# Three of a unit's seven weight blocks: low part by a negated copy and an accumulating DMA; group 3's row sum one step later

## The chip, the core and the metric

The kernel runs on one core of one Trainium2 chip. A core has a matrix engine (TensorE, PE in the profile), three engines for elementwise work (VectorE or DVE, ScalarE or ACT, GpSimd or POOL), an engine that only issues transfers (SyncE or SP), and 16 DMA engines. Each of these works through its own queue in program order and waits on semaphores for the others; the kernel's author places every instruction by hand. A transfer is issued from SP's queue or from POOL's.

The metric is the device time of one execution in microseconds (us). The kernel before takes 1879.46 us (median of 3 runs, 1878.98 to 1880.03).

## The reference

One layer of a backbone on 2048 tokens of 1024 channels, in float32: a gated short convolution, then a mixture of 16 experts with expert-choice routing.

```python
m_l = (silu_c @ ada_w[i] + ada_b[i])[:, None, :]
sh1, sc1, g1, sh2, sc2, g2 = jnp.split(m_l, 6, axis=-1)
hl = modulate(rms_norm(lat, norm_g[i, 0]), sh1, sc1)
gate_b, gate_c, v = jnp.split(hl @ w_in, 3, axis=-1)
yl = (gate_b * dwconv_centred(gate_c * v, conv_w)) @ w_out
lat = lat + g1 * yl
hl2 = modulate(rms_norm(lat, norm_g[i, 1]), sh2, sc2)
lat = lat + g2 * expert_choice_ffn(hl2, moe_router[i], moe_w_gate[i], moe_w_up[i], moe_w_down[i])
```

The change lies in the first half: in the product `hl @ w_in`, and in the six vectors `sh1` to `g2` (the modulation), each the product of one vector with a 1024x1024 matrix, called groups 0 to 5 in the kernel.

## The kernel before

**Split operands.** A float32 factor is held as two tiles, a high part (the rounded value, written as float32r) and a low part (the value minus its high part). A product is three matmuls: high x high, low x high, high x low. Every weight tile therefore has a high part, made by ACT as a copy (L225, L784), and a low part, made by DVE as a subtraction (L235, L785).

**Channel loop, the first half of the tokens.** The loop at L860 runs 14 steps, i = 0 to 13; a step is one group of 128 channels for one quarter (512 tokens) of the first half, with 8 values of k and 9 matmuls each, into three PSUM banks (`in_mm`). Six banks are shared, so a step's banks are needed again two steps later, after `in_out` has emptied them. Between the values of k other work is placed by hand:

- `in_out` (L493) empties the previous step's banks: ACT copies (`cs`), DVE multiplies, POOL copies two columns of the carry, ACT and DVE do the convolution, POOL stores to DRAM.
- `split_to` makes the high and low parts of the next weight pieces (L225, L235), and each low part frees a raw buffer, for which SP then issues the next load (L200). There are three raw buffers.
- `ada_step(g, t)` (L671) does one step of the modulation of group g: at t = 0 to 7 it loads slices of the matrix (`ada_load`, tile `aw`, L528), at t = 1 to 8 DVE adds a slice times a scalar to `acc` (L540; the first by L538), and at t = 9 `ada_end` (L544) sums `acc` over the partitions by four matmul instructions with a matrix of ones (L547). In steps 0 to 4, after every odd k, comes first group 5, t = 0 to 9, then group 3, t = 0 to 9. All these loads are issued from POOL's queue. Group 3's row sum is the last one, at i = 4, k = 7.
- After step 3 `constants` makes the constants of the later routing: some 60 small operations on POOL.
- `x_step` is 5: in steps 5 and 8 the third and fourth quarter of x are loaded into the four large buffers (`b4`) that the modulation also uses, and normalised; in step 6 (`save_full`), 9 and 10 (`save_sums`) they are turned, and sums and differences of quarters are stored to DRAM (`fscr`). At the end of step 11 `load_full` begins to load these back (`fu`), through the same four buffers, in the order of `halves`; `refill` splits them into high and low parts in steps 12 and 13 and in the first four unit steps, and loads the next.

**Unit stage, the second half of the tokens.** The products for the second half are done by a scheme of seven products in place of eight (as in Strassen's): a unit takes two pieces of weights, a and b, each with two halves, and seven half-size products of blocks with the stored sums. There are 12 units, 84 unit steps. A block (`make_block`, L770) is made four unit steps before it is used (`AHEAD`). Blocks 0, 1, 4 and 6 are the halves b1, a0, a1 and b0 as they stand; blocks 2, 3 and 5 are sums, which DVE first writes over a half in place: block 2 over b1 (L778), block 3 over b1 again (L780), block 5 over a0 (L782), and with it b0 is replaced too (L783). After block 5 piece a's buffer is free, and after block 6 that of b (`piece_done`, L762), and SP issues the load of the third piece from there (L200): the buffer that a leaves takes the next unit's b. `unit_step` (L826) does the 12 matmuls of a block (L794 to L796) and empties the banks; a later block of the same unit is added into a bank after ACT has copied it out (L841).

In this stage groups 2 and 4 of the modulation run, one `ada_step` every fourth unit step, with their loads on POOL's queue, as are the convolution's stores.

Of the kernel before, what the change touches and what calls it, by code (L numbers as in the profile page):

```python
# [7 lines left out]
F32 = mybir.dt.float32  # L8
# [4 lines left out]
AF = mybir.ActivationFunctionType  # L13
ALU = mybir.AluOpType
# [8 lines left out]
KD = D // P  # L23
# [17 lines left out]
def dram(src, offset, ap):  # L41
    return bass.AP(tensor=src.tensor, offset=src.offset + offset, ap=ap)
# [3 lines left out]
def block_kernel(ctx: ExitStack, tc, x, c, ada_w, ada_b, norm_g, w_in, conv, w_out, router, wg, wu, wd, out):  # L46
    nc = tc.nc
# [195 lines left out]
    def split_to(i, eng=None):  # L243
        while n_done <= min(i, len(pieces) - 1):
            split_low(n_done, eng)
# [112 lines left out]
    with tc.tile_pool(name="mix", bufs=1) as mix, ExitStack() as ctx_mixd:  # L358

        def b4(name, shape=[P, D]):  # L360
            return mix.tile(shape, F32, name=name, tag="b4", bufs=4)

        def hl_tile(shape, dt=F32R, name="hl"):
            return mix.tile(shape, dt, name=name, tag="hl", bufs=18)
# [22 lines left out]
        def load_x(q, b0=0, b1=4):  # L387
            xq.setdefault(q, [])
            pair_ = None
            for b in range(b0, b1):  # L390
                if q == 1:
                    pair_ = big_tile([P, 2, D], F32, "xt") if b % 2 == 0 else pair_
                    t = pair_[:, b % 2]
                else:
                    t = b4("xt")
                nc.sync.dma_start(t, x[0, q * QT + b * P:q * QT + (b + 1) * P, :])
                xq[q].append(t)
# [16 lines left out]
        def scale_x(q, k):  # L414
            pt, full = pt_hl.pop((q, k)), m2("full")
            t = hl[q, k] = hl_tile([P, 2, QT])
            nc.scalar.activation(t[:, 0], pt, AF.Identity, scale=A1[:, k:k + 1], bias=sh1[:, k:k + 1])  # L417
            nc.scalar.activation(full, pt, AF.Identity, scale=A1[:, k:k + 1], bias=sh1[:, k:k + 1])
            return full
# [4 lines left out]
        def to_hl(q, k):  # L424
            turn_x(q, k)
            low_x(q, k, scale_x(q, k))
# [94 lines left out]
        def bcast_load(dst, src, off, eng=nc.sync):  # L521
            eng.dma_start(dst, dram(src, off, [[0, P], [1, D]]))
# [3 lines left out]
        def ada_load(g, k, eng=nc.sync):  # L526
            ada_in[g, k] = b4("aw")
            eng.dma_start(ada_in[g, k], ada_w[0, k * P:(k + 1) * P, g * D:(g + 1) * D])  # L528

        def ada_add(g, k, dst=None):  # L530
            t = ada_in.pop((g, k))
            if dst is None:
                if k == 0:
                    ada_dst[g] = g2b if g == 5 else b4("dst")
                dst = ada_dst[g]
            if k == 0:
                ada_acc[g] = b4("acc")
                nc.vector.tensor_scalar(ada_acc[g], t, s_col[:, 0:1], None, op0=ALU.mult)  # L538
            else:
                nc.vector.scalar_tensor_tensor(ada_acc[g], t, s_col[:, k:k + 1], ada_acc[g], op0=ALU.mult, op1=ALU.add)  # L540
            if k == 0:
                bcast_load(dst, ada_b, g * D)

        def ada_end(g, dst):  # L544
            for h in range(2):
                pt = tp.tile([P, QT], F32, name="pt", tag="tp")
                nc.tensor.matmul(pt, ones_f, ada_acc[g][:, h * QT:(h + 1) * QT], start=True, stop=True)  # L547
                nc.vector.tensor_add(dst[:, h * QT:(h + 1) * QT], pt, dst[:, h * QT:(h + 1) * QT])
            if g == 4:
                nc.vector.scalar_tensor_tensor(dst, dst, 1.0, ada_g.pop(), op0=ALU.add, op1=ALU.mult)  # L550
            if g < 5:
                nc.gpsimd.dma_start(rows[g - 2:g - 1], dst[0:1])

        def new_banks():
            return [mm.tile([P, QT], F32, name="pm", tag="mm") for _ in range(3)]
# [69 lines left out]
        for g in range(4):  # L625
            k = 2 * g
            more_g = g < 3
            ada_fix(g, 0)
            full = scale_x(0, k)
# [9 lines left out]
            full = scale_x(0, k + 1)  # L639
# [31 lines left out]
        def ada_step(g, t):  # L671

            if t == KD + 1:
                ada_end(g, ada_dst[g])
            if 0 < t <= KD:
                ada_add(g, t - 1)
            if (g, t) == (4, KD):
                ada_g.append(b4("gt"))
                bcast_load(ada_g[0], norm_g, D, nc.gpsimd)
            if t == 0:  # L680
                ada_load(g, 0, nc.gpsimd)
            if t + 1 < KD:
                ada_load(g, t + 1, nc.gpsimd)

        T4, B11, T1, T2, B21, T3, B22 = range(N_GROUP)
        group_of_k = {(2, 0): B11, (2, 1): B21, (3, 1): B22}
# [72 lines left out]
        def raw_half(i, h):  # L759
            return raws[i][:, 4 * h:4 * h + 4]  # L760

        def piece_done(i):  # L762
            nonlocal n_high, n_done
            raws.pop(i)
            n_high = n_done = i + 1
            load_to(i + depth())
# [3 lines left out]
        def make_block(n):  # L770

            u, i = divmod(n, N_GROUP)
            a, b = first_s + 2 * u, first_s + 2 * u + 1
            t = blk[n] = hl_tile([P, 2, KD // 2, P], name="sb")
            p, h = ((b, 1), (a, 0), (b, 1), (b, 1), (a, 1), (a, 0), (b, 0))[i]
            full = raw_half(p, h)
            if i == 2:
                nc.vector.tensor_add(full, raw_half(b, 0), full)  # L778
            elif i == 3:
                nc.vector.tensor_sub(full, full, raw_half(a, 0))  # L780
            elif i == 5:
                nc.vector.tensor_sub(full, full, raw_half(b, 0))  # L782
                nc.vector.tensor_sub(raw_half(b, 0), raw_half(a, 1), raw_half(b, 1))  # L783
            nc.scalar.activation(t[:, 0], full, AF.Copy)  # L784
            nc.vector.tensor_sub(t[:, 1], full, t[:, 0].bitcast(F32))  # L785
            if i > 4:
                piece_done(p)

# [67 lines left out]

        end_plain = w_chan[0, KD - 1, 2]
        steps = [(ct, q) for ct in range(KD) for q in range(2) if q or ct > 1]
        x_step = 5
        for i, (ct, q) in enumerate(steps):  # L860
            in_out(*pend)
            if i == 5:
                for t in cnts:
                    nc.vector.tensor_copy(t, zero1.to_broadcast([P, 4]))
            nxt = w_chan[0, ct, 2]
            split_to(min(end_plain, nxt + (1 if q % 2 == 0 else 3)))
            if i in (x_step, x_step + 3):
                load_x(2 if i == x_step else 3)
            last_i = len(steps) - 1
            ps = new_banks()  # L870
            for k in range(KD):
                in_mm(ps, q, W_chan(0, ct), k)
                if (ct, q) == (0, 1) and k + 3 < KD:
                    to_hl(1, k + 3)
                if i in (x_step, x_step + 3) and k in (2, 3, 4, 5):
                    norm_x(2 if i == x_step else 3, k - 2)
                if i == x_step + 1 and k % 2 == 1:
                    save_full(2, k // 2)
                if i == x_step + 3 and k == 7:
                    load_other(0)  # L880
                if i in (x_step + 4, x_step + 5) and k in (1, 5):
                    j = 2 * (i - x_step - 4) + k // 4
                    save_sums(j)
                    if j < 3:
                        load_other(j + 1)
                if i < x_step and k % 2 == 1:
                    t = 4 * i + k // 2
                    ada_step(*((5, t) if t < KD + 2 else (3, t - KD - 2)))
                if i == last_i - 2 and k == 7:
                    for s in range(4):  # L890
                        load_full(s)
                if i == last_i - 1:
                    if k in (1, 2, 4, 5, 7):
                        refill((1, 2, 4, 5, 7).index(k))
                    if k in (3, 6):
                        make_block((3, 6).index(k))
                if i == last_i:
                    if k in (1, 2, 3, 6, 7):
                        refill(5 + (1, 2, 3, 6, 7).index(k))
                    if k in (4, 5):  # L900
                        make_block(k - 2)
            pend = (ps, q, ct)
            if i == 3:
                before, ones_b, tri, slot_r, step, bias, need, zero1, cnts, aux, same, quick = constants(m2)
                nc.sync.dma_start(rt, dram(router, 0, [[E, P], [E * P, KD], [1, E]]))
                nc.scalar.activation(rts[:, :, 0], rt, AF.Copy)
                nc.vector.tensor_sub(rts[:, :, 1], rt, rts[:, :, 0].bitcast(F32))
# [22 lines left out]
        for n in range(n_steps):  # L930
            u, i = divmod(n, N_GROUP)
# [6 lines left out]
            if n >= 6 and n % 4 == 2:  # L938
                t = n // 4 - 1
# [701 lines left out]
```

## Time and profile before

| | |
|---|---|
| median of 3 runs | 1879.46 us |
| the profiled execution | 1880.41 us |
| its span in the profile | 1878.2 us |
| mean granted clock of TensorE in it | 0.986 |
| channel loop with its first part | up to about 324 us |
| unit stage | 324 to 557 us |

The span is the time from the first to the last instruction in the trace; the execution's own time lies 2.2 us above it. Two stretches of 40 us, one from the channel loop and one from the unit stage, show how the engines stand there: the length, then for PE, weight loads, DVE, ACT and POOL the busy us and the number of instructions, then the granted clock, the share of the DMA engines and GB/s.

```profile
160.00:200.00 40.00, 34.62 (x146) 27.14 (x147) 14.93 (x22) 12.16 (x18) 9.15 (x20) 0.88 0.40 129
...
400.00:440.00 40.00, 40.00 (x177) 32.94 (x177) 32.30 (x43) 15.75 (x26) 2.82 (x9) 1.00 0.35 106
```

In the first PE is idle for 5.4 us and the clock is below full; in the second PE is never idle, DVE is busy for 32 of 40 us, ACT for 16 and POOL for 3. How to read the other views: a row of the timeline has the start, the duration, the engine, the line, the operation, the tile written and the tiles read, and in brackets the idle time of the engine before it and what ended that; a row of the waits has the total, the number and the longest.

### The profile page before, as it was taken

What the parts mean: (1) busy time and instruction counts of PE and PEld (TensorE: products, weight loads), DVE (VectorE), ACT (ScalarE), POOL (GpSimd) and SP (SyncE); (2) the same over time, 40 slices, a digit from 0 to 9 for tenths busy, and PEclk for the clock granted to TensorE, in tenths of its full rate; (3) what the DMA queues carried; (4) which work ended last, traced back from release to release, by engine and by line L of the source; (5) the groups of instructions that cost most, each with busy time, mean ns of one, the idle gap of its engine ahead of it and who ended that gap; (6) DMA issues with size and microseconds to landing.
All of it is one profiled execution on the core that took longest, in us unless ns stands there. A gap on an engine that the chain in (4) does not pass through costs nothing.

```text
span 1878.2 us, 29302 instructions
## 1 busy us (share of the span) xinstructions
PE 1813.7 (97%) x11511; PEld 1609.9 (86%) x11511; DVE 1218.5 (65%) x1722; ACT 872.2 (46%) x1154; POOL 320.4 (17%) x494
## 2 busy tenths in 40 slices
PE   7998999999999999499999999999999999999998
PEld 6786888888878887398999999999999999999997
DVE  6554346777776677788666665765666576566653
ACT  5511234433344556466454554555455455444542
POOL 1223231010002222300202111210210121021002
PEclk9998999999999999799999999999999999999999
DMA  9353466434448888385778778787877978888774
GB/s 335 114 187 123 133 216 201 125 116 135 135 153 250 241 264 252 112 258 186 228 242 258 226 236 258 223 238 234 258 234 225 261 221 242 241 251 231 223 230 87
DMA packets 304634, 393.67 MB, mean 210 GB/s; under 512 B 102724, under 2 KB 173680, under 8 KB 304496
## 3 DMA queue, kind: packets, MB, share of 16 engines
q1 hardware_dynamic: 280032, 305.77, 53.3%
q0 software_dynamic: 24464, 86.03, 15.5%
q8 instruction: 90, 1.47, 0.3%
q14 instruction: 48, 0.39, 0.1%
HBM read 311.52 MB, written 57.68 MB: 197 GB/s over the span
## 4 chain that ended last, share of the span: by engine, by line
PE 87%; DVE 5%; DMA 3%; ACT 2%; issue 2%; POOL 1%; SPq 0%; POOLq 0%; DVEq 0%; ACTq 0%
PE pm L1464 12%; PE pm L1466 12%; PE pm L1468 12%; PE pm L1533 6%; PE pm L1531 6%; PE pm L1532 6%; PE pm L794 4%; PE pm L796 4%; PE pm L795 4%; PE pm L488 4%; PE pm L489 4%; PE pm L491 3%; PE pm L993 3%; PE pm L996 3%; PE pm L994 3%
## 5 line engine op out<-in xcount | busy, mean ns | idle before, releaser
L235 DVE TENSOR_TENSOR ws<-raw,ws 128x1024 fp32r<-128x1024 f32 x408 | 484.9, 1221 | 279.6 <-ACT ws L225 279.6
L225 ACT ACTIVATE ws<-raw 128x1024 fp32r<-128x1024 f32 x408 | 412.5, 1051 | 412.4 <-PE pm L1468 322.9
L1466 PE MATMUL pm<-xT,ws 128*128 128x256 f32 x2048 | 566.2, 276 | 1.9 <-DVE xT L1444 1.8
L1464 PE MATMUL pm<-xT,ws 128*128 128x256 f32 x2048 | 567.6, 277 | 0.0
L1468 PE MATMUL pm<-xT,ws 128*128 128x256 f32 x2048 | 565.9, 276 | 0.0
L1466 PEld LDWEIGHTS pm<-xT,ws 128*128 128x128 f32 x2048 | 384.6, 188 | 3.9 <-DVE xT L1444 2.1
L1464 PEld LDWEIGHTS pm<-xT,ws 128*128 128x128 f32 x2048 | 384.8, 188 | 1.6 <-ACT xT L1443 0.3
L1468 PEld LDWEIGHTS pm<-xT,ws 128*128 128x128 f32 x2048 | 384.5, 188 | 0.0
L1561 POOL DMA_INDIRECT out_dram<-ot,idx x30 | 104.9, 3497 | 586.8 <-DVE ot L1550 582.8
L1533 PE MATMUL pm<-ws,hT 128*128 128x512 f32 x504 | 198.4, 394 | 0.0
L1531 PE MATMUL pm<-ws,hT 128*128 128x512 f32 x504 | 198.3, 393 | 0.0
L1532 PE MATMUL pm<-ws,hT 128*128 128x512 f32 x504 | 197.1, 391 | 0.0
L488 PE MATMUL pm<-hl,ws 128*128 128x512 f32 x384 | 154.5, 402 | 0.5 <-ACT hl L417 0.5
L489 PE MATMUL pm<-hl,ws 128*128 128x512 f32 x384 | 150.7, 392 | 0.0
L794 PE MATMUL pm<-tg,sb 128*128 128x512 f32 x336 | 131.8, 392 | 0.6 <-ACT cx L841 0.5
L795 PE MATMUL pm<-tg,sb 128*128 128x512 f32 x336 | 130.8, 389 | 0.0
L796 PE MATMUL pm<-tg,sb 128*128 128x512 f32 x336 | 130.7, 389 | 0.0
L1533 PEld LDWEIGHTS pm<-ws,hT 128*128 128x128 f32 x504 | 94.7, 188 | 20.1
L1532 PEld LDWEIGHTS pm<-ws,hT 128*128 128x128 f32 x504 | 94.7, 188 | 19.8
L1531 PEld LDWEIGHTS pm<-ws,hT 128*128 128x128 f32 x504 | 94.7, 188 | 18.7
L491 PE MATMUL pm<-hl,ws 128*128 128x512 f32 x384 | 108.8, 392 | 0.0
L993 PE MATMUL pm<-ws,hl 128*128 128x512 f32 x256 | 102.4, 400 | 0.8 <-ACT hl L924 0.8
(360 smaller groups left out, 2483.6 us busy)
## 6 DMA issues: line engine op xcount, KB each, us to landing
raw<-in_moe_w_down_dram SPq DMA_DIRECT2D x128, 512.0 KB, 4.6
raw<-in_moe_w_gate_dram SPq DMA_DIRECT2D x126, 512.0 KB, 4.8
raw<-in_moe_w_up_dram SPq DMA_DIRECT2D x126, 512.0 KB, 4.1
raw<-in_sc_w_in_dram SPq DMA_DIRECT2D x42, 512.0 KB, 4.5
xt<-in_x_dram SPq DMA_DIRECT2D x32, 512.0 KB, 6.5
aw<-in_ada_w_dram POOLq DMA_DIRECT2D x32, 512.0 KB, 4.3
hl<-in_ada_w_dram SPq DMA_DIRECT2D x32, 256.0 KB, 6.3
hl<-vscr SPq DMA_DIRECT2D x16, 512.0 KB, 4.8
```

The costliest lines, as they stand in the source:

```text
L225: nc.scalar.activation(t[:, 0], raws[n_high], AF.Copy)
L235: (eng or nc.vector).tensor_sub(t[:, 1, ..., s], raw[..., s], t[:, 0, ..., s].bitcast(F32))
L488: nc.tensor.matmul(ps[m], wh, t[:, 0], start=(k == 0), stop=False)
L489: nc.tensor.matmul(ps[m], wl, t[:, 0], start=False, stop=False)
L794: nc.tensor.matmul(o, t[:, 0, j], r[:, 0], start=(first and j == 0), stop=False, skip_group_check=True)
L795: nc.tensor.matmul(o, t[:, 1, j], r[:, 0], start=False, stop=False, skip_group_check=True)
L1464: nc.tensor.matmul(o, w[:, 0, j, c0], xT[:, 0, k], start=(k == 0 and f % 2 == 0), stop=False, skip_group_check=True)
L1466: nc.tensor.matmul(o, w[:, 0, j, c0], xT[:, 1, k], start=False, stop=False, skip_group_check=True)
L1468: nc.tensor.matmul(o, w[:, 1, j, c0], xT[:, 0, k], start=False, stop=(k == KD - 1), skip_group_check=True)
L1531: nc.tensor.matmul(ps[s], h, w[:, 0, j], start=(k == 0), stop=False)
L1532: nc.tensor.matmul(ps[s], h, w[:, 1, j], start=False, stop=False)
L1533: nc.tensor.matmul(ps[s], l, w[:, 0, j], start=False, stop=(k == KD - 1))
```

## The change

Three things are changed.

1. `make_block`: for i = 0, 1 and 4 DVE's subtraction goes. ACT writes the negated high part into the low part's place, and a DMA from POOL's queue adds the raw half to it, within SBUF. Block 6 and the three sums keep the subtraction.
2. `ada_step`: the loads of groups 3 and 5 are issued from SP's queue; those of groups 2 and 4 stay on POOL's.
3. Group 3's row sum (t = 9) moves from i = 4, k = 7 to i = 5, k = 5, and `x_step` from 5 to 6, so that loading, normalising, `save_full` and `save_sums` of the third and fourth quarter each come one step later. `load_full` and `refill` stay where they are.

```diff
@@ ada_step
+            eng = nc.gpsimd if g in (2, 4) else nc.sync
             if t == 0:
-                ada_load(g, 0, nc.gpsimd)
+                ada_load(g, 0, eng)
             if t + 1 < KD:
-                ada_load(g, t + 1, nc.gpsimd)
+                ada_load(g, t + 1, eng)
@@ make_block
             nc.scalar.activation(t[:, 0], full, AF.Copy)
-            nc.vector.tensor_sub(t[:, 1], full, t[:, 0].bitcast(F32))
+            if i in (0, 1, 4):
+                nc.scalar.activation(t[:, 1], t[:, 0].bitcast(F32), AF.Copy, scale=-1.0)
+                nc.gpsimd.dma_start(t[:, 1], full, accum_op=ALU.add)
+            else:
+                nc.vector.tensor_sub(t[:, 1], full, t[:, 0].bitcast(F32))
             if i > 4:
                 piece_done(p)
@@ channel loop
-        x_step = 5
+        x_step = 6
...
-                if i < x_step and k % 2 == 1:
+                if i < 5 and k % 2 == 1:
                     t = 4 * i + k // 2
-                    ada_step(*((5, t) if t < KD + 2 else (3, t - KD - 2)))
+                    if t < 2 * KD + 3:
+                        ada_step(*((5, t) if t < KD + 2 else (3, t - KD - 2)))
+                if i == 5 and k == 5:
+                    ada_step(3, KD + 1)
```

One `if k == 0` of `ada_add` is written as two, which changes no instruction.

More of the change, by code (lines that the diff above doesn't have):

```diff
@@ L537, in ada_add @@
                 ada_acc[g] = b4("acc")
+            if k == 0:
                 nc.vector.tensor_scalar(ada_acc[g], t, s_col[:, 0:1], None, op0=ALU.mult)
```

## The prediction

> **What bounds the kernel now.** The page comes first: the share of each engine, and the granted clock in 40 slices.
>
> ```profile
> span 1878.2 us, 29302 instructions
> ...
> PE 1813.7 (97%) x11511; PEld 1609.9 (86%) x11511; DVE 1218.5 (65%) x1722; ACT 872.2 (46%) x1154; POOL 320.4 (17%) x494
> ...
> PEclk9998999999999999799999999999999999999999
> ```
>
> TensorE (PE) is busy 97% of the span. VectorE (DVE) has a third of its time free, so work taken from DVE is worth only what PE waits for it. The second view is the table of PE's own waits, for the two stages that the change touches: 80 to 330 us (first two lines) and 320 to 560 us (third line). Columns: who waited for whom, total us, times, longest.
>
> ```profile
> PE pt L547 <- DVE acc L540: 8.0, 1, 8.0
> PE pt L412 <- DVE xt L405: 0.9, 1, 0.9
> ...
> PE pm L794 <- ACT cx L841: 0.5, 1, 0.5
> ```
>
> In the channel loop PE stands still once for 8.0 us, at group 3's row sum. In the unit stage, where the weight blocks are made, it waits 0.5 us in all. The timeline of the four engines shows where the 8.0 us come from.
>
> ```profile
> 152.61 0.73 ACT L505 ACTIVATE y<-u,v_col 128x512 f32<-128x512 f32 x1 [11.89 <-POOL u L500]
> 156.75 2.60 DVE L540 SCALAR_TENSOR_TENSOR acc<-aw,s_col,acc 128x1024 f32<-128x1024 f32 x2
> 158.33 0.54 POOL L528 DMA_DIRECT2D aw<-in_ada_w_dram  x1 [0.26 <-DVE acc L540]
> 163.16 1.28 DVE L540 SCALAR_TENSOR_TENSOR acc<-aw,s_col,acc 128x1024 f32<-128x1024 f32 x1 [3.81 <-DMA aw<-in_ada_w_dram]
> 164.50 3.78 PE L547 MATMUL pt<-acc,ones_f 128*128 128x512 f32 x4 [8.00 <-DVE acc L540]
> ```
>
> POOL makes constants until 152 us, so ScalarE's (ACT's) `y` starts 11.89 us late, DVE's adds stand behind `y`, the last load of group 3 starts at 158.33, and PE, done with step 4 at 164.50 - 8.00 = 156.5, gets its sum at 164.5. Short windows give the clock (length, PE busy, instructions, granted clock, DMA share, GB/s):
>
> ```profile
> 155.00:160.00 5.00, 1.49 (x7) 0.92 0.52 149
> 160.00:165.00 5.00, 0.50 (x1) 0.50 0.36 113
> 165.00:170.00 5.00, 5.00 (x10) 0.56 0.00 0
> ```
>
> The clock falls to 0.50 in the gap and is 0.56 on average in the 5 us after it.
>
> **The change, part by part.** *The row sum a step later.* The last add ends at 163.16 + 1.28 = 164.4 even with the times of before. Steps of the channel loop are 16.3 us long (the three `cs` rows below), so k = 5 of step 5 ends at 156.5 + 6/8 x 16.3 = 168.7: 4.3 us of cover, and the 8.0 us go. The four matmuls of the sum took 3.78 us at the low clock; undisturbed they take 1.72 (chain of waits, below): 2.0 more. A mean of 0.56 over 5 us is half speed up to 169.4, so the first matmuls of step 5 lost about 0.5. The wait of 0.9 for `xt` should go too: its loads now follow a step that nothing delays. Together 11.4 us. Late next is `in_out` of step 4's banks, behind the last add on DVE: some 3.5 us of operations, done near 168, and its banks are wanted at 156.5 + 16.3 + 1.7 = 174.5. The loads of groups 5 and 3 now stand on SP's queue behind weight loads, which wait for subtractions (L235) that stand ahead of the same adds on DVE anyway: I cost that at nothing; if the cover went, the 4.3 us would bear it.
>
> *x_step 6: the hand-over to the units.* The whole x chain moves a step towards the end, and with it the last `save_sums`, now in step 11, whose final store (T4) `load_full(1)` must wait for. Template: the same store in step 10 of before, then medians of issue to landing, then the `cs` of steps 12, 13 and of the first unit.
>
> ```profile
> 280.01 0.54 POOL L723 DMA_DIRECT2D fscr<-fy  x1
> ...
> fscr<-fy POOLq DMA_DIRECT2D x4, 256.0 KB, 4.0
> fu<-fscr SPq DMA_DIRECT2D x14, 512.0 KB, 4.9
> ...
> 291.31 0.60 ACT L498 ACTIVATE cs<-pm 128x512 f32<-128x512 f32 x1 [7.91 <-PE pm L491]
> 307.63 0.60 ACT L498 ACTIVATE cs<-pm 128x512 f32<-128x512 f32 x1 [5.53 <-PE pm L491]
> 324.01 0.60 ACT L498 ACTIVATE cs<-pm 128x512 f32<-128x512 f32 x1 [2.24 <-PE pm L491]
> ```
>
> Step 11 of before began at 291.31 - 16.3 = 275.0, so the store is issued 5.0 us into the next step, lands 4.0 later, and `load_full(1)`, at 4.5 for one load (4.9 is for bunches), lands 13.5 us into step 12's 16.3. Queued behind it: SP's next loads, and on ACT and DVE the refills, two blocks and `in_out`. Placing these one after the other at their durations, ACT is 4.1 us late at the start of step 13 and DVE 2.8 us late when block 5 is done in the first unit. PE has spare banks until then. But block 5 frees the raw buffer whose next load ACT awaits ahead of a copy that PE needs (chain of waits, first unit):
>
> ```profile
> 338.15 0.49 ACT cx L841
> 338.69 0.50 PE pm L794
> ```
>
> That copy was already 0.5 us late. It becomes 2.8 + 0.6 (one more ACT operation ahead of it) = 3.4 us later.
>
> *The blocks.* Per unit three subtractions leave DVE, three negated copies come to ACT and three accumulating DMAs to POOL. Median durations are the middle of three (ns):
>
> ```profile
> L784 ACT ACTIVATE sb<-raw x84: 611/624/635, 296.1 to 544.5; 128x512 fp32r<-128x512 f32 x84
> L785 DVE TENSOR_TENSOR sb<-raw,sb x84: 676/692/695, 298.0 to 547.3; 128x512 fp32r<-128x512 f32 x84
> ```
>
> That is 36 x 0.69 = 25 us less on DVE and 36 x 0.62 = 22 us more on ACT, beside matmuls and by themselves worth nothing. What counts is a loop. Block 0 reads the upper half of raw piece b; block 2 overwrites that half (L778) and must now wait until block 0's DMA has read it. Block 2 leads to 3, 4 and 5, block 5 frees a buffer, and the load into it is the next unit's b. ACT's first block operation after each load, and DVE's L778 (first and last of ten such pairs, then the eleventh load):
>
> ```profile
> 336.48 0.63 ACT L784 ACTIVATE sb<-raw 128x512 fp32r<-128x512 f32 x1 [2.18 <-DMA raw<-in_sc_w_in_dram]
> 340.39 0.69 DVE L778 TENSOR_TENSOR raw<-raw 128x512 f32<-128x512 f32 x1
> ...
> 509.28 0.63 ACT L784 ACTIVATE sb<-raw 128x512 fp32r<-128x512 f32 x1 [1.88 <-DMA raw<-in_sc_w_in_dram]
> 512.95 0.69 DVE L778 TENSOR_TENSOR raw<-raw 128x512 f32<-128x512 f32 x1
> 529.03 0.63 ACT L784 ACTIVATE sb<-raw 128x512 fp32r<-128x512 f32 x1 [2.64 <-DMA raw<-in_sc_w_in_dram]
> ```
>
> Load to load: (529.03 - 336.48)/10 = 19.26 us; load to L778, mean of the ten, 3.86; the rest 15.40. PE's own pace, from two copies that waited for it a unit apart, is 493.14 - 474.10 = 19.04:
>
> ```profile
> 474.10 0.69 DVE L843 TENSOR_TENSOR cx<-cx,pm 128x512 f32<-128x512 f32 x1 [0.88 <-PE pm L796]
> ...
> 493.14 0.69 DVE L843 TENSOR_TENSOR cx<-cx,pm 128x512 f32<-128x512 f32 x1 [0.68 <-PE pm L796]
> ```
>
> So the loop has next to no room. Afterwards load to L778 is two ACT operations (1.24), a hand-over from an engine to POOL's issue (278.01 - 277.72 = 0.29, rows below), the DMA's time d from issue to landing, and some 0.07 of waking: 1.6 + d. The rest loses block 4's subtraction, 0.6 of DVE's queue: 14.8. Loop: 16.4 + d. Behind the waiting L778 stand, on DVE, blocks 2 and 3, the row sums of groups 2 and 4, and L845 to L847, whose bank PE wants two blocks (5.4 us) into the next unit; with L778 1.2 us later than now that still holds. Block 4's DMA, which the load of the next b must await too, has from block 4 to the end of block 5. On POOL, `aw` loads and the convolution's stores stand behind the DMAs; nothing before the row sums waits for them. No row shows an accumulating DMA inside SBUF. The rows near it, with landings in us (min/median/max):
>
> ```profile
> 277.03 0.69 DVE L716 TENSOR_TENSOR tsum<-fx,fy 128x512 f32<-128x512 f32 x1 [6.33 <-ACT cs L498]
> 278.01 0.54 POOL L717 DMA_DIRECT2D fscr<-tsum  x1 [0.75 <-DVE tsum L716]
> ...
> L516 POOL DMA_DIRECT2D vscr<-y x8: 539/554/653, 68.4 to 312.3; - x8
> ...
> DMA to landing us min/median/max: 2.3/2.4/2.7
> ...
> L1495 POOL DMA_INDIRECT out_dram<-ot,tbits x5: 1549/1562/1563, 1859.6 to 1870.2; - x5
> ...
> DMA to landing us min/median/max: 3.7/4.3/5.0
> ...
> out_dram<-ot,idx POOLq DMA_INDIRECT x30, 7.9
> ```
>
> Below, a plain store of the same size from POOL's queue: 2.3; adding cannot be quicker than storing. Above, the accumulating scatters of twice the size among heavy traffic: 7.9, less the longer issue (1.56 - 0.54), 6.9. Nearest are the quiet accumulating scatters of 256 and 128 KB: 4.3 - 1.0 = 3.3. I take **d = 3.5**, 0.2 more for the 512 KB load that crosses it.
>
> *The sum of the unit stage.* The first load is 2.8 us late, 15.3 us after the stage's start (324.0) instead of 12.5; the eleventh lands at 15.3 + 10 x (16.4 + 3.5) = 214.3. PE reaches unit 10 at 493.14 - 13.6 (five of seven blocks) + 2 x 19.04 = 517.6, that is 193.6 after the stage's start, and wants ACT's copy another 13.6 later, after group 4's row sum:
>
> ```profile
> 528.47 1.72 PE pt L547 x4
> ```
>
> 193.6 + 13.6 + 1.72 = 208.9, less three ACT operations (1.7): the load may land at 207.2. Loss: 214.3 - 207.2 = 7.1; in general 10 d - 27.9, and never under the 3.4 of the first unit. **Sum: 11.4 - 7.1 = 4.3 us faster.** The profiled execution (1880.41, of which 1878.2 is the span) would come to 1876.1, the median of the runs, 1879.46, to **1875.2**.
>
> **The rivals.** *The loop is hidden* (d up to 3.1): only the 3.4 us of the first unit are lost, 8.0 gained, 1871.5. For it: the plain stores at 2.4. Against: the accumulating scatters. The Trainium skill, "DMA: Bandwidth & Descriptors", section "Anatomy of one DMA — SWDGE (gpsimd) path", gives about 2.0 us plus the bytes over 436 GB/s for a DMA from this queue: for 256 KB an estimate of 2.6 us, which is this rival. The plain stores agree with it (2.4); the page's fit has no adding.
>
> *The loop sets the pace outright* (slower). The accumulating DMA is the mechanism, between block 0 and block 2 of each unit; each us of d costs 10. It decides at d = 3.9 (no gain) and 4.3 (over 0.2% slower): at 5.1, midway between 3.3 and 6.9, the loss is 23.1 and the time 1891. For it: the loop has no slack of its own, and the crowded scatters. Against: the quiet ones.
>
> *Given back at the hand-over*: `load_full(1)` lands 3 to 5 us later than placed, or the row sum is not freed as the change says (its 4.3 us of cover eaten by SP's queue). Either leaves about 1879.
>
> *POOL's issues wait out DVE's operations.* If each issue waited for a subtraction (0.69), d is 4.2, the loss 14.1 and the time 1882; behind longer ones it would be slower still. The loads that POOL issues in this stage speak against it, at 530 ns with one at 1627:
>
> ```profile
> L528 POOL DMA_DIRECT2D aw<-in_ada_w_dram x32: 527/530/1627, 78.2 to 499.6; - x32
> ```
>
> The Trainium skill, "SBUF — State Buffer", section "Who interferes with whom", has such a lock for DVE's two-port modes, and says a tensor_tensor has none; by that the rival falls, and the row agrees.
>
> **How the numbers follow.** Forecast (d between 3.1 and 4.0) 0.42, hidden 0.14, slower 0.26, given back 0.14, POOL held 0.04. A measurement of this kernel tells about 0.2% (3.8 us) from no change. Faster by more: hidden, and the forecast up to d = 3.55 (0.30): 0.44. Slower: 0.26 and half of POOL held: 0.28. Within: the rest, 0.28. The range goes from 1870 (hidden, with a smaller hand-over loss) to 1889 (d = 4.9), which leaves out the crowded scatters' end.
>
> **What would show it.** The row sum's four matmuls without a wait and near 1.7 us, and no fall of the clock at 155 to 170: the 11.4. L778 released by a DMA and not by ACT or DVE, 1.6 + d after the load; load-to-load times near 19.9 us: the loop. PE's waits before L795 and L796 or on ACT's L841 in the unit stage: the loss; none there, and the first rival holds. `fu` loads late in step 12 and one PE wait of 3 us in the first unit: the hand-over. I am wrong in the mechanism if DVE's L778 still waits for nothing, and wrong in the size if d lies outside 3.1 to 4.0.

## The result, and the profile after

The changed kernel takes 1894.26 us (median of 4 runs, 1891.76 to 1894.72), the kernel before 1879.38 beside it: a ratio of 1.0076, 95% interval 1.0059 to 1.0094. It is slower, by some 15 us, and outside the range of the prediction.

From here on the lines of the changed kernel count: the row sum is L548, block 2's sum L780, ACT's high part L786, its negated copy L788, the accumulating DMA L789, the matmuls of a block L800 to L802, the copy of a bank L847.

First the page of the changed kernel: engines, clock in 40 slices, the chain of work that ended last by line, and the group of the high product (count, busy us, mean ns, then idle us before it and for whom).

```profile
span 1892.1 us, 29374 instructions
...
PE 1819.7 (96%) x11511; PEld 1612.5 (85%) x11511; DVE 1198.5 (63%) x1686; ACT 893.0 (47%) x1190; POOL 338.5 (18%) x514
...
PEclk9999999999999999799999999999999999999999
...
PE pm L1473 11%; PE pm L1475 11%; PE pm L1477 11%; PE pm L1542 6%; PE pm L1540 6%; PE pm L1541 6%; PE pm L488 3%; PE pm L489 3%; PE pm L491 3%; PE pm L1002 3%; PE pm L1003 3%; PE pm L1005 3%; DMA sb<-raw 2%; DMA raw<-in_sc_w_in_dram 1%; DMA tr<-xs 1%
...
L800 PE MATMUL pm<-tg,sb 128*128 128x512 f32 x336 | 135.2, 402 | 15.3 <-ACT cx L847 15.2
```

DVE has lost 20 us of work (1218.5 to 1198.5) and the kernel has become slower. The fourth slice of the clock has risen from 8 to 9, and in the chain stands a transfer inside SBUF, `sb<-raw`: the new DMA itself.

The stages, by the first matmul of the unit stage and ACT's first split of the next product behind it (before: 323.98 and 557.14 us; after: 313.85 and 570.16). The channel loop ends 10.1 us sooner; the unit stage takes 256.3 us in place of 233.2, 23.1 more; what follows takes 1321.9 in place of 1321.1. Sum: -10.1 + 23.1 + 0.9 = 13.9, the difference of the spans.

*The channel loop.* PE's waits from 80 to 330 us, the timeline of PE and short windows of the changed kernel (windows: length, busy us and instructions of PE, weight loads, DVE, ACT, POOL, then granted clock, DMA share, GB/s):

```profile
PE pm L800 <- ACT cx L847: 2.9, 1, 2.9
PE pt L548 <- DVE acc L541: 0.8, 1, 0.8
PE pt L412 <- DVE xt L405: 0.4, 1, 0.4
...
169.57 1.88 PE L548 MATMUL pt<-acc,ones_f 128*128 128x512 f32 x4
...
160.00:165.00 5.00, 5.00 (x23) 4.14 (x23) 2.68 (x4) 1.58 (x3) 0.00 (x0) 1.00 0.09 34
165.00:170.00 5.00, 5.00 (x23) 3.94 (x22) 3.88 (x7) 1.04 (x2) 1.09 (x2) 1.00 0.31 88
```

Group 3's row sum no longer waits (no bracket behind it), takes 1.88 us, and the clock stays at 1.00 where it was 0.50 and 0.56.

*The unit stage as a whole*, before, then after:

```profile
324.00:557.10 233.10, 232.49 (x1017) 190.36 (x1015) 177.49 (x233) 89.01 (x145) 21.40 (x54) 1.00 0.42 130
```

```profile
313.80:570.20 256.40, 240.43 (x1017) 192.41 (x1016) 161.53 (x205) 111.08 (x185) 51.22 (x89) 0.98 0.60 155
```

The same 1017 recorded matmuls. PE's idle time rises from 0.6 to 16.0 us (256.40 - 240.43), 15.4 more; the busy time rises by 7.9, and the mean clock falls from 1.00 to 0.98. The DMA engines are busy 60% instead of 42%. Who waits for whom in that stage of the changed kernel, PE from 315 to 590 us, DVE and ACT from 320 to 570:

```profile
PE pm L800 <- ACT cx L847: 15.2, 9, 3.5
...
DVE raw L780 <- DMA sb<-raw: 37.3, 10, 6.0
DVE cx L849 <- PE pm L802: 25.1, 11, 4.6
...
ACT sb L786 <- DVE raw L780: 42.4, 11, 6.4
ACT sb L786 <- DMA raw<-in_sc_w_in_dram: 30.7, 10, 6.4
```

Read as a ring: DVE's block 2 waits for the new DMA in ten of the units, ACT's block 2 for DVE, ACT's next block 0 for the load, and PE for the copy that stands behind that block on ACT. No engine is busy all the way round the ring; it is made of DVE's and ACT's operations on the blocks, of hand-overs, and of two transfers, the new DMA and the weight load.

The ring's length, from the timeline of the changed kernel (first and last unit, then a long and a short pass between them):

```profile
328.03 0.63 ACT L786 ACTIVATE sb<-raw 128x512 fp32r<-128x512 f32 x1 [1.10 <-DMA raw<-in_sc_w_in_dram]
543.03 0.63 ACT L786 ACTIVATE sb<-raw 128x512 fp32r<-128x512 f32 x1 [3.62 <-DMA raw<-in_sc_w_in_dram]
...
410.48 0.57 POOL L528 DMA_DIRECT2D aw<-in_ada_w_dram  x1 [8.52 <-DVE acc L541]
411.21 0.86 POOL L789 DMA_DIRECT2D sb<-raw  x1 [0.15 <-issue]
417.26 0.69 DVE L780 TENSOR_TENSOR raw<-raw 128x512 f32<-128x512 f32 x1 [5.19 <-DMA sb<-raw]
...
458.76 0.90 POOL L789 DMA_DIRECT2D sb<-raw  x1 [6.52 <-ACT sb L788]
460.99 0.88 POOL L528 DMA_DIRECT2D aw<-in_ada_w_dram  x1
462.29 0.69 DVE L780 TENSOR_TENSOR raw<-raw 128x512 f32<-128x512 f32 x1 [6.03 <-DMA sb<-raw]
```

Load to load is (543.03 - 328.03)/10 = 21.50 us, against 19.26 before and 19.04 for PE. Block 0's DMA, from its issue to the start of L780, takes 417.26 - 411.21 = 6.05 us in the long pass and 3.53 in the short one; over the ten units of the ring 3.51, 4.23, 4.49, 5.12, 6.05, 4.79, 3.53, 5.98, 7.00 and 4.09, **4.88 on average**. In the long pass a 512 KB load (`aw`) was issued 0.73 us ahead of it, in the short one 2.2 us behind it. In the three units of the ten where such a load was issued at most 1.5 us ahead, the DMA took 6.05, 5.98 and 7.00; in the other seven 4.25 on average. The DMA view for 405 to 420 us (40 slices of 0.375 us: busy tenths of the 16 engines, then what was issued and its us to landing) shows the crowd:

```profile
DMA  0000059999200179999935679999999731000000
...
aw<-in_ada_w_dram POOLq DMA_DIRECT2D x1, 512.0 KB, 5.4
sb<-raw POOLq DMA_DIRECT2D x2, 256.0 KB, 6.0
```

From about 410 to 417 the engines are busy for 70% or more in all but three of the slices, with `aw` and two accumulating DMAs at once.

### The profile page after: what moved, and what is told of

Read it like the earlier page. It is cut to its first block, busy times and chain, and to the rows that moved or that the text cites. A ratio compares the mean times of both kernels' runs of the same rounds, so it can differ in the third digit from the quotient of the medians.

```text
span 1892.1 us, 29374 instructions
## 1 busy us (share of the span) xinstructions
PE 1819.7 (96%) x11511; PEld 1612.5 (85%) x11511; DVE 1198.5 (63%) x1686; ACT 893.0 (47%) x1190; POOL 338.5 (18%) x514
## 4 chain that ended last, share of the span: by engine, by line
PE 75%; DMA 7%; DVE 7%; issue 5%; ACT 3%; POOL 1%; SPq 0%; POOLq 0%; DVEq 0%; ACTq 0%
PE pm L1473 11%; PE pm L1475 11%; PE pm L1477 11%; PE pm L1542 6%; PE pm L1540 6%; PE pm L1541 6%; PE pm L488 3%; PE pm L489 3%; PE pm L491 3%; PE pm L1002 3%; PE pm L1003 3%; PE pm L1005 3%; DMA sb<-raw 2%; DMA raw<-in_sc_w_in_dram 1%; DMA tr<-xs 1%
## 5 line engine op out<-in xcount | busy, mean ns | idle before, releaser
L800 PE MATMUL pm<-tg,sb 128*128 128x512 f32 x336 | 135.2, 402 | 15.3 <-ACT cx L847 15.2
L801 PE MATMUL pm<-tg,sb 128*128 128x512 f32 x336 | 132.6, 395 | 0.7 <-DMA sb<-raw 0.7
L802 PE MATMUL pm<-tg,sb 128*128 128x512 f32 x336 | 132.3, 394 | 0.0
```

## The experiments

Edits are against the changed kernel unless it is said otherwise. The kernel before took 1879.53 us beside r1 to r4, 1880.13 beside r5 to r8, 1879.47 beside r9 and r10.

**r1: everything but the blocks.** `make_block` as before; the row sum, the queues and `x_step` as changed.

```diff
@@ make_block
-            if i in (0, 1, 4):
-                nc.scalar.activation(t[:, 1], t[:, 0].bitcast(F32), AF.Copy, scale=-1.0)
-                nc.gpsimd.dma_start(t[:, 1], full, accum_op=ALU.add)
-            else:
-                nc.vector.tensor_sub(t[:, 1], full, t[:, 0].bitcast(F32))
+            nc.vector.tensor_sub(t[:, 1], full, t[:, 0].bitcast(F32))
```

> The changed kernel with the old make_block: all seven low parts by VectorE's subtraction, no accumulating DMA; the loads on SP's queue, the later row sum and x_step 6 stay. Loop theory (block 0's DMA holds block 2 back, and the loop load - block 0 - block 2 - block 5 - next load becomes longer than PE's unit): the unit stage takes about 233 us again, as before, plus at most 3 us in its first unit; PE begins it near 314 us; time 1868 to 1872. If the later x work were what costs, the time stays above 1885.

Measured: 1872.81 us, 0.8 above the range expected, ratio 0.9962 (0.9950 to 0.9975). The unit stage went from 313.52 to 550.20, 236.7 us, with one wait of over 1 us left in it, the hand-over:

```profile
PE pm L796 <- ACT cx L843: 2.7, 1, 2.7
```

The half of the change that moves the row sum is worth 7 us; all the loss is in the blocks.

**r2: the blocks alone.** The kernel before with only the new `make_block`.

> The kernel before with the new make_block alone (blocks 0, 1 and 4 by negated copy and accumulating DMA). Loop theory: the unit stage grows by some 20 us and the 8 us of group 3's row sum stay, so 1896 to 1903. If the loss came from the moved x work, 1880.

Measured: 1895.59 us, 0.4 below the range expected, ratio 1.0084 (1.0067 to 1.0100). PE's row sum waits its old 7.9 us, and in the unit stage (323.43 to 578.28, 254.9 us) the ring is back:

```profile
PE pt L547 <- DVE acc L540: 7.9, 1, 7.9
...
PE pm L798 <- ACT cx L845: 13.3, 11, 2.7
```

**r3: block 0 alone by DMA, r4: blocks 1 and 4 alone.**

```diff
@@ r3
-            if i in (0, 1, 4):
+            if i == 0:
@@ r4
-            if i in (0, 1, 4):
+            if i in (1, 4):
```

> The changed kernel with the DMA for block 0 alone; blocks 1 and 4 by subtraction again. Loop theory: block 0 is the one whose half block 2 overwrites, so nearly all of the loss stays: 1886 to 1896, VectorE's add of block 2 waits for the DMA 3 to 6 us in most units. If the loss goes with the number of ScalarE operations and DMAs (rival: ScalarE's queue or POOL's queue is overloaded), a third of it stays: 1876 to 1880.

> The changed kernel with the DMA for blocks 1 and 4; block 0 by subtraction again. Loop theory: block 2 waits for no DMA, the loop is as long as before or 0.6 us shorter per unit, and the time is that of the run without DMA, 1868 to 1872. Rival (number of operations): two thirds of the loss stay, 1884 to 1888.

Measured: r3 1894.49 us, ratio 1.0087 (1.0069 to 1.0105); r4 1873.30, 0.9974 (0.9960 to 0.9987), 1.3 above its range. PE's waits in the unit stage of r3, then of r4 with its landings:

```profile
PE pm L800 <- ACT cx L847: 15.5, 12, 3.1
```

```profile
PE pm L800 <- ACT cx L847: 2.8, 1, 2.8
...
L789 POOL DMA_DIRECT2D sb<-raw x24: 865/882/926, 300.0 to 532.4; - x24
...
DMA to landing us min/median/max: 3.3/3.3/6.2
```

One of the three DMAs costs nearly everything. Twice as many of the same kind, at a place where nobody waits for them, cost nothing against r1. So it is neither the negated copies on ACT nor POOL's issues, nor the DMA as such, but block 0's place.

**r5: block 0's DMA without the ring.** All three DMAs stay. The sum of blocks 2 and 3 is written to a tile of its own, so that L780 need not wait until the DMA has read the half b1. Block 6 is computed from the half b1 as it stands, in place of the sum, so the output differs from the reference in that block.

```diff
-        blk = {}
+        blk, sum_of = {}, {}
...
             if i == 2:
-                nc.vector.tensor_add(full, raw_half(b, 0), full)
+                sum_of[u] = hl_tile([P, KD // 2, P], F32, "bsum")
+                nc.vector.tensor_add(sum_of[u], raw_half(b, 0), full)
+                full = sum_of[u]
             elif i == 3:
+                full = sum_of.pop(u)
                 nc.vector.tensor_sub(full, full, raw_half(a, 0))
```

> The changed kernel with all three DMAs, but block 2's sum is written to a tile of its own (from the 18 buffers of the blocks) and block 3 made from that, so that nothing overwrites the half which block 0's DMA reads. Loop theory: VectorE's add waits for no DMA, load to load falls from 21.5 to PE's 19.0 to 19.3 us, the unit stage takes 236 to 240 us, time 1871 to 1876. Rivals: if the DMAs hurt by landing too late for PE, or by their traffic, the time stays at 1890 or above.

Measured: 1873.54 us, ratio 0.9971 (0.9959 to 0.9983), although the DMAs landed after 3.3 to 7.9 us, much as in the changed kernel. DVE's waits in the unit stage no longer name the DMA, and PE has two waits there, of which the longer, 3.6 us, is the hand-over:

```profile
PE pm L803 <- ACT cx L850: 3.9, 2, 3.6
```

The cost was the wait of L780.

**r6: the loads off POOL's queue.** All the modulation's loads from SP, to see whether POOL's order lengthens block 0's DMA.

```diff
@@ ada_step
-            eng = nc.gpsimd if g in (2, 4) else nc.sync
+            eng = nc.sync
```

> The changed kernel with the loads of groups 2 and 4 on SP's queue too, so that no 512 KB load stands ahead of block 0's DMA in POOL's queue. In the changed kernel that DMA took 4.9 us from issue to VectorE's add on average: about 6.3 in the three units with such a load just ahead of it, about 4.1 to 4.3 in the others. If the load ahead makes the difference: mean near 4.2, load to load near 20.8, some 7 us less, time 1886 to 1889. If the DMA is slow for other reasons, the time stays within 3 us of 1894.

Measured: 1901.83 us, ratio 1.0110 (1.0094 to 1.0125). The expectation failed: block 0's DMA became longer, 5.86 us on average, and SP, which issues the weight loads, now stands behind the modulation (SP's waits, 320 to 570 us):

```profile
SPq L528 <- DVE acc L541: 58.7, 10, 16.2
```

In six of the ten passes SP issued an `aw` load 1.1 to 1.9 us ahead of block 0's DMA; these took 6.57 us on average, the other four 4.78. So a neighbour from another queue goes with a longer DMA just as one from POOL's queue does, and SP issued one just ahead more often than POOL had (six passes against three). The Trainium skill, "DMA: Bandwidth & Descriptors", section "Rules for kernel authors", says that spreading transfers over SP, ACT and GpSimd does not help, since all run on the same 16 engines and interleave; this run agrees (6.57 us beside a load from SP's queue, 4.78 without one so near).

**r7 and r8: the hand-over mended.** r1 and r4 with the fourth quarter of x taken in step 8 again, the third staying in step 6.

```diff
-        x_step = 6
+        x_step, x_last = 6, 8
...
-            if i in (x_step, x_step + 3):
+            if i in (x_step, x_last):
...
```

> Low parts by VectorE as in the first run, and the fourth quarter of x loaded in step 8 as before the change instead of step 9, so that its sums are stored in steps 9 and 10. The row sum's gain stays (unit stage begins near 314), the wait of 2.7 us at the hand-over to the units goes: 1868 to 1871. If that wait has another cause, 1872 to 1874 as in the first run.

> As the run beside it, with blocks 1 and 4 by negated copy and DMA. Loop theory: these two are off the loop, so the same time within 1.5 us: 1868 to 1871. If DMA traffic or ScalarE's queue mattered, 1874 or more.

Measured: r7 (subtractions by DVE) 1870.12 us, ratio 0.9942 (0.9929 to 0.9956); r8 (blocks 1 and 4 by DMA) 1868.10, 0.9933 (0.9919 to 0.9946). The hand-over's wait is 0.6 us in r7 and gone in r8. The two intervals overlap, so whether the two harmless DMAs gain anything is not settled; r8 is the fastest kernel of the study, 11 to 12 us ahead of the kernel before and 26 ahead of the changed one.

**r9: the ring opened, with block 6 from the sum.** r8 with block 0 by DMA too; the sum of blocks 2 and 3 has a tile of its own as in r5, and lives there until block 5 has used it. The edit is against r8, without the lines that r5 has already.

```diff
-            if i in (1, 4):
+            if i in (0, 1, 4):
...
-                nc.vector.tensor_sub(raw_half(b, 0), raw_half(a, 1), raw_half(b, 1))
+                nc.vector.tensor_sub(raw_half(b, 0), raw_half(a, 1), sum_of.pop(u))
```

> The kernel of r8 with block 0's low part by the accumulating DMA as well, but with the sum of blocks 2 and 3 written to a tile of its own, so that the rounding of block 5 is the last to need the DMA and nothing of the next unit's load waits for it. If the closed loop from the load through the DMA of block 0 to the next load is what cost the time, and not the DMA as such, the units stay at PE's pace: 1866 to 1871 us, within 3 us of r8 (1868.1), with loads about 19 us apart whatever the DMA takes to land (3.3 to 7 us). If the late low part of block 0 itself holds up the matmuls, or three such DMAs of a unit crowd the others out, it is at 1885 or more with PE waiting at the high product again.

Measured: 1872.13 us, ratio 0.9960 (0.9948 to 0.9972): 1.1 above the range expected and 4.0 above r8 where at most 3 were expected, but far below the rival's 1885. The intervals of r8 and r9 do not overlap, so r9 is the slower of the two. In its profiled execution the unit stage is that of a kernel without a ring, at full clock, with DMAs that land after 3.3 to 8.3 us; L781, the sum, starts 19.2 and 19.0 us apart and waits for nothing:

```profile
312.75:545.42 232.67, 232.50 (x1017) 190.39 (x1015) 157.79 (x200) 112.26 (x179) 52.05 (x87) 1.00 0.65 168
...
327.77 0.68 DVE L781 TENSOR_TENSOR bsum<-raw 128x512 f32<-128x512 f32 x1
346.98 0.69 DVE L781 TENSOR_TENSOR bsum<-raw 128x512 f32<-128x512 f32 x1
366.02 0.69 DVE L781 TENSOR_TENSOR bsum<-raw 128x512 f32<-128x512 f32 x1
```

Its stage ends at 545.42, r8's at 545.41, so in these two executions the difference to r8 (3.3 us of span) lies in later stages that the edit does not touch, part of it in a stretch (845 to 945 us) with a clock of 0.97 against r8's 1.00. Why these differ is open.

**r10: the other loads taken away.** The changed kernel without the loads of groups 2 and 4; their additions read another tile, so these two row vectors are other numbers.

```diff
@@ ada_load
+            if g in (2, 4):
+                ada_in[g, k] = g2b
+                return
```

> The changed kernel without the 512-KB loads of groups 2 and 4 (their additions read a tile that is there already, so the row vectors of these two groups are other numbers; the same instructions run on the engines). If those loads in flight are what lengthens block 0's DMA from 3.4 us to 4.9 us and more, its mean from issue to the addition falls to about 4.0 us or below, the loads of the units come 20.5 us apart instead of 21.5, and the time is 1884 to 1888 us. If the DMA takes its 4.9 us whatever else is in flight, the time is within 3 us of 1894.

Measured: 1882.23 us, ratio 1.0009 (0.9998 to 1.0021), 12 us less than the changed kernel and 2 below the range expected. Waits of PE and DVE in the unit stage, first and last load, and landings (L783 is this kernel's sum of block 2, L803 its high product):

```profile
PE pm L803 <- ACT cx L850: 8.3, 9, 3.2
...
DVE raw L783 <- DMA sb<-raw: 28.4, 10, 5.0
...
327.70 0.63 ACT L789 ACTIVATE sb<-raw 128x512 fp32r<-128x512 f32 x1 [1.17 <-DMA raw<-in_sc_w_in_dram]
531.67 0.63 ACT L789 ACTIVATE sb<-raw 128x512 fp32r<-128x512 f32 x1 [3.69 <-DMA raw<-in_sc_w_in_dram]
...
DMA to landing us min/median/max: 3.3/3.5/6.2
```

Block 0's DMA takes 4.25 us on average (expected about 4.0), the loads come 20.40 us apart (expected 20.5). So the loads of groups 2 and 4 stand for 0.63 us (4.88 - 4.25) of the 1.48 by which the mean exceeds the quiet 3.4, less than half. In r3, without the DMAs of blocks 1 and 4, the mean is 4.59, that is 0.29 less. The rest is not shown by any run: the weight loads and the stores stayed in all of them. Other traffic is the likely cause, since the longest pass of r10, 5.84 us, again had a 512 KB load (`dst`, a bias) issued 1.75 us ahead of it. The edit also takes away waits on POOL and DVE, which it cannot tell from the traffic; the ring, 16.4 + 4.25 = 20.65, needs none of them.

## Why the prediction was wrong

The ring can be checked over all the kernels that have it: its length by the prediction's form against what the loads show, and the loss 10 d - 27.9 against the unit stage's length less 233.2.

| kernel | mean d | 16.4 + d | load to load | 10 d - 27.9 | stage longer by |
|---|---|---|---|---|---|
| changed | 4.88 | 21.3 | 21.50 | 20.9 | 23.1 |
| r2, blocks alone | 5.12 | 21.5 | 21.61 | 23.3 | 21.7 |
| r6, loads on SP | 5.86 | 22.3 | 22.50 | 30.7 | 34.1 |
| r10, no other loads | 4.25 | 20.6 | 20.40 | 14.6 | 12.5 |

(r3 keeps block 4's subtraction on DVE, so that 0.6 us come back into the ring: 17.0 + 4.59 = 21.6, measured 21.53.)

1. *The row sum a step later: right, 1.3 us too large.* Predicted 11.4, measured 10.1. The 8.0 us and the slow clock behind them went as worked out. What is missing is a wait of 0.8 us at group 5's row sum, whose loads SP now issues, and 0.4 of the 0.9 for `xt`, which stayed: 1.2 together. The queue of SP was costed at nothing. The first wait is not there in r2, where POOL issues these loads as before; in the other kernels with SP's loads it is between nothing (r3, r4) and 0.7 us (r5, r8).
2. *The hand-over: right in its cause and nearly in its size, not in its place.* `load_full(1)` landed 13.6 us into step 12 (predicted 13.5), and block 5's sum in the first unit (L784) came 2.8 us later after the stage's start than before, as predicted. PE then waited 2.9 us (predicted 3.4), but two blocks sooner than predicted. The step "PE has spare banks until then" failed: ACT waited 3.17 us for that sum, and the first copy of a bank, which PE wanted, stood behind it (timeline of ACT; 324.39 is the copy). r7 and r8 made the wait 0.6 and nothing.

```profile
294.84 1.06 ACT L745 ACTIVATE tg<-fu 128x1024 fp32r<-128x1024 f32 x1 [5.36 <-DMA fu<-fscr]
...
322.91 0.63 ACT L786 ACTIVATE sb<-raw 128x512 fp32r<-128x512 f32 x1 [3.17 <-DVE raw L784]
...
324.39 0.58 ACT L847 ACTIVATE cx<-pm 128x512 f32<-128x512 f32 x1
```

3. *The ring: right in its place and its form.* L780 is released by a DMA, the first leg is 6.5 us (1.6 + 4.88), the second 15.0 (predicted 14.8), and PE waits at the copy, as the prediction's list of signs said. Block 4's DMA, which the next load must await too, does not set the length: in ten of the eleven units timed SP issues that load 0.02 to 0.03 us after block 5's low part is done. r5 and r9 show that it is L780's wait that costs: with the sum in a tile of its own, r5 takes the time of r1 (1873.54 and 1872.81 us), and r9's unit stage is as long as r8's (232.7 and 232.2 us).
4. *The size of d: wrong.* The step that failed is the term "I take d = 3.5, 0.2 more for the 512 KB load that crosses it." The first half holds: in its quiet passes the DMA takes 3.4 to 3.5, and the quiet accumulating scatters (3.3) were the right row for these. The second half was taken as one crossing load with a price of 0.2. In the trace three of ten passes have an `aw` load issued just ahead and take 6 to 7 us, and the mean is 4.88. The prediction placed `aw` on POOL's queue behind the DMAs and not in the DMA engines beside them. That is part of it: without these loads d is still 4.25 (r10), and what else lengthens it is open. A sign of crowding stood in the prediction's own rows: plain stores of the same size from the same queue took 2.4 us in one row and 4.0 in another (`fscr<-fy`), and only the first was weighed for d. At ten passes each 0.1 us of d is 1 us of time: 1.4 us of d are 14 of the 19 us by which the forecast missed. The rest is 1.3 from the first point, 2.2 that the stage lost beyond the formula (its cause is open), 0.9 in the later stages, and the difference between the profiled execution and the medians. With d = 4.88 the prediction's own sum gives 1879.5 - 11.4 + 20.9 = 1889.0, the upper end of its range; these smaller terms carry the time 5 us beyond it.
5. *The rivals.* "The loop sets the pace outright" is what happened, on the mechanism and close to the price that it named (1891 at d = 5.1; that d was not quite reached, and the smaller terms above made up for it). It had a chance of 0.26 because the range of d was weighed by its quiet rows. "POOL's issues wait out DVE's operations" falls: an issue takes 0.86 to 0.91 us in nearly every unit. "The loop is hidden" needed d up to 3.1, which no DMA of any run showed: the shortest landing is 3.2 us (r2).

The Trainium skill, "DMA: Bandwidth & Descriptors", section "Anatomy of one DMA — SWDGE (gpsimd) path", has the fit that gave the estimate of 2.6 us for the 256 KB; the quiet accumulating DMA measured 3.3. The same page, section "Rules for kernel authors", says that an accumulating DMA reads its destination and writes it later; with the bytes counted twice its fit would be an estimate of 3.2, near the quiet value, and neither covers the 4.88 among other loads.

## What to carry to other kernels

Here a DMA that took over an engine's work kept its source locked until it had landed. Before an operand is handed to a DMA, look for the next instruction that overwrites it, and follow that one around until the ring closes. The ring of the kernel before (19.26 us) was within 0.3 us of the pace of PE (19.04), so the work saved on DVE was worth nothing and every added microsecond was paid once per unit. In such a case take the transfer's duration from the crowded rows, not from the quiet ones, and multiply it by the number of passes. The cure that worked in r5 and, in the unit stage, in r9 is a tile of its own for the overwriting result, the one in r4 and r8 is to give the DMA only those operands that nobody overwrites soon. Whether the DMAs then gain anything over plain subtractions is not settled (r7 and r8).

## What the runs showed that was not expected

- The accumulating DMA inside SBUF takes POOL 0.88 us to issue, where a plain 256 KB store took 0.54 in the kernel before, and lands after 3.3 us at best (3.2 in r2). In the changed kernel:

```profile
L789 POOL DMA_DIRECT2D sb<-raw x36: 857/879/1226, 297.4 to 553.0; - x36
...
DMA to landing us min/median/max: 3.3/3.9/8.5
```

- A factor of 2.5 lies between the quickest and the slowest landing of the same 256 KB in one kernel, while the DMA engines are on average 60% busy. A mean share says little about what one transfer meets.
- A gap of PE costs more than its length, but not each one does. In the changed kernel's unit stage the clock was 0.50 right behind the two longest gaps (2.86 us, ended at 325.03; 3.46 us, ended at 459.00) and stayed at 1.00 behind the next ones (2.70 us, ended at 428.14; 2.33 us at 517.37):

```profile
325.03 0.80 PE L800 MATMUL pm<-tg,sb 128*128 128x512 f32 x1 [2.86 <-ACT cx L847]
428.14 0.50 PE L800 MATMUL pm<-tg,sb 128*128 128x512 f32 x1 [2.70 <-ACT cx L847]
...
325.00:328.00 3.00, 2.97 (x7) 2.40 (x8) 2.58 (x3) 1.93 (x3) 0.00 (x0) 0.50 0.67 195
428.00:434.00 6.00, 5.74 (x24) 4.43 (x24) 4.70 (x6) 2.75 (x7) 0.10 (x1) 1.00 0.50 146
459.00:463.00 4.00, 4.00 (x9) 3.13 (x10) 0.69 (x1) 1.09 (x2) 2.10 (x3) 0.50 0.71 123
```

The length of a gap alone does not decide this. In r6 the clock was 0.50 for 3 us behind a gap of only 2.23 us (ended at 529.19); in r2 it was 0.50 behind one of 2.65 us (437.44) and 1.00 behind one of 2.68 us (414.60). What does decide it is not shown. In the changed kernel the clock was 0.50 from 325 to 328, 0.95 to 331, 0.50 from 459 to 463 and 0.87 to 470: 3 x 0.50 + 3 x 0.05 + 4 x 0.50 + 7 x 0.13 = 4.6 of the stage's 7.9 us of longer matmuls.
